# An early ScalarE table load, smaller room bounds in the first mixer, and a final norm in place

## The chip, the cores and the metric

The kernel runs on one core of a Trainium2 chip, in one launch. The metric is the device time of that launch in microseconds (us). Inputs are laid out for the kernel on the host before the launch, and outputs are put back in the reference's order after it.

The core's engines are TensorE (PE in the profile, with PEld for its weight loads), VectorE (DVE), ScalarE (ACT), GpSimd (POOL) and SyncE (SP). SP does no arithmetic here: it issues nearly all transfers. Each engine runs its own list of instructions in order, and a semaphore wait at the head of a list holds everything behind it.

## The reference

One inference step of a two-layer decoder over 512 prompt tokens and 8 × 8 sample tokens, 576 columns in all, with model width 1024, in float32:

```
layer 0: x += mixer_A_and_B(rmsnorm(x))      # pooling mixer and gated DeltaNet, one input and one output projection
layer 1: x += dilated_window_attention(rmsnorm(x))
each layer: x += attention_into_256_memory_tokens(rmsnorm(x)); x += conv_ffn(rmsnorm(x))
y = rmsnorm(x, g_final) = x * rsqrt(mean(x*x) + 1e-6) * g_final
```

The outputs are y and the new states and caches. Of this the change touches the loading of x at the very start, the order of work in layer 0's mixer, and the last line.

## The kernel before

**Layout.** Activations lie transposed: the 1024 channels are 8 tiles of 128 partitions, and the 576 tokens are columns. `x` is two buffers of four tiles each, [128, 4 × 576]. Work goes in two halves of the columns, `HALF = ((0, 256), (256, 320))`: half 0 is 256 columns wide, half 1 is 320.

**Dense layers.** `dense` multiplies streamed weights with an activation held as two rounded parts, so each product takes three matmuls: high × high, high × low, low × high. A weight unit is 128 × 1024 elements, 512 KB: loaded by SP into `wr` (2 buffers), copied to `wh` by ACT, its remainder put into `wl` by DVE (4 buffers each). The callback `evac` takes each result out of PSUM. After every few matmuls `dense` calls `tick()`; a piece of work handed to `later(n, f)` is emitted n ticks on. At the program's end `flush()` emits what is still pending, in order.

**The norm that follows a residual add.** `res_evac` adds PSUM to `x` on DVE and calls `_Next.put(k, hf)`. That squares the tile on ACT and sums squares on DVE (`squares`). After the eighth tile `sums` adds over the partitions with PE (a product with a matrix of ones), takes the diagonal and the inverse root on DVE in small instructions, and `rows` spreads the result over all partitions with PE and copies it from PSUM to SBUF on ACT as `R`.

**The end.** The last down projection of layer 1 works its final four units with half 1 ahead of half 0. `rows` then calls `final(R, hf)`. For each of 8 tiles it makes `y = x * g * R` in a fresh buffer `y` from the arena: either one DVE instruction or an ACT scaling and a POOL product, and SP sends each tile out on its own. Half 1's tiles are spread over later ticks, in steps of four; half 0's are emitted at once.

**The start.** `build` sets `eps` with DVE, issues the load of the small vectors `vecs` from ACT's queue, then from SP: `x` half 0 (two transfers of four tiles), two weight units, `x` half 1 (two transfers), and constants. ACT then scales and rounds each tile of half 0 (`parts`), casts the two weight units, does the same for half 1 and then squares.

**The arena.** Nearly all buffers come from a software allocator, `_Arena`, over 16 pages: 2 of 4608 elements a partition, and 14 of 2304. A page holds float32 or rounded buffers, not both. `room()` counts free elements. The lanes below count idle pages, a page of 4608 as two. The allocator runs when the program is laid out, on the host, so on the chip these conditions set only the order of instructions and which buffers share an address.

**Layer 0's mixer.** `sched` interleaves five lanes with a filler, in an order planned from a table of engine costs. The filler is the input projection's remaining columns (`cols`), then the projection of the memory tokens (`kv`), then half of the output projection (`outp`). Lanes: `first` (tokens, gates, scan), `second` (preparation of later chunks), `third` (sample tokens; it writes 8 state tiles `o_ss`), `fourth` (rounds the pooling mixer's result into `mh` and `ml`, which `outp` multiplies) and `fifth` (the same for the scan's result, into `oh` and `ol`, which the second half of the output projection multiplies). Some lanes wait for room:

```
second:  "pool" in st or self.room() > PROOM
fourth:  "kv" in st or "mem" in st and idle() >= MXPAGES
fifth:   "outp" in st or idle() >= FPAGES
kv:      idle pages >= KVPAGES
```

`"mem"` is set when the memory tokens have been rounded, `"kv"` when their whole projection has been emitted. The pooling mixer's product `pool_mm` is emitted when the planner holds its operands ready, or after its patience of `POOLW` ticks.

Of the kernel before, what the change touches and what calls it, by code (L numbers as in the profile page):

```python
# [11 lines left out]
AF = mybir.ActivationFunctionType  # L12
OP = mybir.AluOpType
# [3 lines left out]
NEG = -1e30  # L17
L = {'k0': 6.0, 'k3': 2.0, 'k1': 3.0, 'k2': 5.0, 't0': 3.0, 't1': 0.5, 't2': 0.2, 't3': 1.0, 't4': 0.4, 'g0': 0.4, 'g1': 0.5, 'g2': 8.0, 'g3': 1.0, 'g4': 0.4, 'g5': 1.5, 'g6': 1.0, 'v0': 3.0, 'v1': 0.2, 'p0': 0.0, 'p1': 0.8, 'p2': 0.0, 'p3': 1.0, 'p4': 1.5, 'p5': 0.2, 'p6': 0.8, 'p7': 0.2, 'p8': 0.8, 'p9': 0.0, 'p10': 0.1, 'p11': 0.3, 'o0': 1.2, 'o1': 3.6, 'o2': 0.0, 's0': 0.1, 's1': 0.5, 's2': 0.1, 's3': 0.8, 's4': 0.0, 's5': 0.6, 's6': 0.0, 'm0': 2.8, 'm1': 0.5, 'm2': 1.2, 'm3': 0.5}
CF, SC, CT, CA = 0.11, 0.85, 8, 20
KVPAGES = 4  # L20
MXPAGES = 2
XT = 3
FPAGES = 2
XL = 4, 16
XL1 = 4, 12
MET0 = 0.0, 0.0, 0.0, 0.0
# [3 lines left out]
KT = 8  # L30
NTOK = 576
HALF = ((0, 256), (256, 320))
# [271 lines left out]
SPARE = 2  # L304
AGE = 40
SROOM = 5500
PROOM = 8000
MROOM = 4500
KROOM = 4000
MRAW = 170  # L310
# [1 line left out]
WROOM = 1500  # L312
OUT_LATER = 24
PATIENCE = 60
POOLW = 40
LOAD_LATER = 18
LOW_LATER = 18
QUICK = 3, 5
# [322 lines left out]
class _Next:  # L641
# [8 lines left out]
    def put(self, k, hf):  # L650
        if not self.last:
            self.parts(k, hf)
        self.squares(k, hf)

    def parts(self, k, hf, lag=True):
        p = self.p
# [27 lines left out]
    def rows(self, hf):  # L684
        p = self.p
        t0, N = HALF[hf]
        if self.R is None:
            self.R = p.S([128, NTOK], s="R1")
        p.nc.scalar.copy(self.R[:, t0:t0 + N], p.rstd_rows(self.y[hf], N)[:, :N])
        if self.on_rows is not None:  # L690
            self.on_rows(self.R, hf)
            if hf == 1 and not self.last:
                self.R = None

    def clear(self):
# [6 lines left out]
class _Prog:  # L702
# [37 lines left out]
        bs = [self.S([128, min(4, n - k) * NTOK], dt, s=name) for k in range(0, n, 4)]  # L740
        return [_Cols(bs[k // 4], k % 4 * NTOK, NTOK) for k in range(n)]

    def load_x(self, src, at=(0, NTOK), eng=None):

        t0, N = at
        if self.x is None:
            self.x = self.wide("x", dt=F32)
        for k in range(0, KT, 4):
            b = self.x[k].buf[:].rearrange("p (k t) -> p k t", k=4)
            (eng or self.nc.sync).dma_start(b[:, :, t0:t0 + N], src[k:k + 4, :, t0:t0 + N].rearrange("k p t -> p k t"))  # L750

    def room(self):
        return self.arena.room()
# [287 lines left out]
    def build(self):  # L1041
        nc, aps = self.nc, self.aps
        c = self.cpool
        self.vecs = c.tile([128, NVEC], F32, name="vecs")
        cid = c.tile([128, 256], F32, name="cid")
        self.my = c.tile([128, 2], F32, name="my")
        self.mR = c.tile([128, 256], F32, name="mR")
        self.y4 = c.tile([128, 4], F32, name="y4")
        self.eps = c.tile([128, 1], F32, name="eps")
        nc.vector.memset(self.eps[:], EPS)  # L1050
        self.acc = {}
        nc.scalar.dma_start(self.vecs[:], aps["vec"])
        self.x = None
        self.load_x(aps["x"], HALF[0])
        self.ident, self.ones = cid[:, 0:128], cid[:, 128:256]


        w, w6 = aps["w"], aps["w6"]
        self.pos = {}
        k = 0  # L1060

        def add(name, n):
            nonlocal k
            self.pos[name] = len(self.stream)
            for _ in range(n):
                self.stream.append((w[k], 1024))
                k += 1

        def tail(l):
            add(f"mq{l}", 8)  # L1070
            add(f"mo{l}", 8)
            for ci, (s, n) in enumerate(CHUNKS):
                add(f"up{l}{ci}", 2 * n)
                if n == 8:
                    add(f"dn{l}{ci}", 8)
                else:
                    self.pos[f"dn{l}{ci}"] = len(self.stream)
                    for i in range(8):
                        self.stream.append((w6[l, i], n * 128))

        add("in", 20)
        add("mk0", 8)
        add("mv0", 8)
        add("outp", 4)
        add("outd", 4)
        tail(0)
        for g in range(3):
            add(f"v{g}", 4)
        for hp in range(4):
            add(f"qk{hp}", 6)  # L1090
        add("mk1", 8)
        add("mv1", 8)
        add("outc", 4)
        tail(1)


        self.quick = {i for a, b in (("v0", "qk0"), ("mv0", "outp"), ("mv1", "outc"))
                      for i in range(self.pos[a] + 3, self.pos[b] + 3)}
        self.load_to(self.NR)
        self.load_x(aps["x"], HALF[1])  # L1100
        nc.sync.dma_start(cid[:], aps["c_id"])
        self.Kc, self.Vc = {}, {}
        nx = _Next(self, "g_mix", 0)
        for hf in range(2):
            for kt in range(KT):
                nx.parts(kt, hf, False)
            self.split_to(2)
        nx.lags = START
        for hf in range(2):
            for kt in range(KT):  # L1110
                nx.squares(kt, hf, False)
        self.x = None
        nx = self.layer0(nx)
        if self.stop == "l0mix":
            return self.flush()
        nx = self.mem_stage(0, nx)
        if self.stop == "l0mem":
            return self.flush()
        nn = _Next(self, "g_mix", 8, perm=True, on_rows=self.rope_rows)
        nn.lags = (18, 24), (10, 20)  # L1120
        self.ffn(0, nx, nn)
        if self.stop == "l0":
            return self.flush()
        nx = self.layer1(nn)
        if self.stop == "l1mix":
            return self.flush()
        nx = self.mem_stage(1, nx)
        self.ffn(1, nx, _Next(self, None, 0, on_rows=self.final, last=True))
        self.flush()

    def rope_rows(self, R, hf):
# [5 lines left out]
                self.nc.sync.dma_start(self.cs[n][:], self.aps["c_" + n])  # L1137
            self.nc.gpsimd.tensor_tensor(self.cs[n][:, t], self.cs[n][:, t], R[:, t], op=OP.mult)

    def final(self, R, hf):  # L1140
        nc, aps = self.nc, self.aps
        t0, N = HALF[hf]

        def tile(k):
            y = self.S([128, N], s="y")
            x, g, r = self.x[k][:, t0:t0 + N], self.vec("g_final", k), R[:, t0:t0 + N]
            if k < 5 if hf == 0 else k % 2:
                nc.vector.scalar_tensor_tensor(y[:], x, g, r, op0=OP.mult, op1=OP.mult)
            else:
                nc.scalar.activation(x, x, AF.Copy, scale=g)  # L1150
                nc.gpsimd.tensor_tensor(y[:], x, r, op=OP.mult)
            nc.sync.dma_start(aps["y"][k][:, t0:t0 + N], y[:])

        for i, k in enumerate(((5, 0, 1, 6, 2, 3, 7, 4), range(KT))[hf]):
            if hf:
                self.later(1 + 4 * i, lambda k=k: tile(k))
            else:
                tile(k)


    def layer0(self, nx):
        nc, aps = self.nc, self.aps
# [320 lines left out]
        def second():  # L1483
            yield 0, 0, lambda: "gates" in st
            yield from vtok()
            yield 0, 0, lambda: "pool" in st or self.room() > PROOM
            yield from self.dn_prep(QKV, 1, st)
# [16 lines left out]
        def fourth():  # L1504
            yield 0, 0, lambda: "kv" in st or "mem" in st and idle() >= MXPAGES
            mh.extend(self.wide("xh", 4))
# [4 lines left out]
        def fifth():  # L1511
# [8 lines left out]
            self.dn1 = self.d8 = self.sc = self.gl = None  # L1520
            yield 0, 0, lambda: "outp" in st or idle() >= FPAGES
            oh.extend(self.wide("xh", 4))
# [8 lines left out]
        def kv():  # L1531
            yield 0, 0, lambda: sum(len(p) * n // 2304 for n, p in self.arena.idle().items()) >= KVPAGES
            self.mem_ahead()
# [971 lines left out]
```

## Time and profile before

| what | us |
|---|---|
| median of 3 runs | 2044.92 |
| lowest and highest run | 2040.68, 2045.32 |
| the profiled execution, its own time | 2044.57 |
| span of its trace, first to last instruction | 2042.4 |
| PE busy in that span | 1987.4 |

The profile shows one execution. Times in its rows count from the span's first instruction, so the profiled execution's own time is 2.2 us longer than its span. Nearly every instruction carries the same source line, since one helper emits them all; they are told apart by engine, operation, shape and place in time. Arena buffers all appear as `page`, PSUM as `p`.

### The profile page before, as it was taken

Reading aid. Unit: us, or ns where it says so; the run is one execution under the profiler, and the core shown is the slowest. Engines: PE = TensorE matmul, PEld = TensorE weight load, DVE = VectorE, ACT = ScalarE, POOL = GpSimd, SP = SyncE. Lnnn points to the kernel's source line nnn. Section 1 sums busy time; section 2 is a strip of 40 time slices with the busy share of each in tenths; the row PEclk is TensorE's granted clock in tenths of the full one; section 3 lists DMA queues with packets and bytes.
Section 4 is the critical chain, followed back from the end, with each engine's and each line's share of the span. In section 5 each row is a group of like instructions: output and inputs, shape, how many; then the busy total and the mean of one; then the engine's idle time right before and its main releaser. Section 6 shows DMA issues by size and latency. Waiting matters only on the chain.

```text
span 2042.4 us, 40671 instructions
## 1 busy us (share of the span) xinstructions
PE 1987.4 (97%) x16443; PEld 1849.4 (91%) x16443; DVE 1252.5 (61%) x3020; ACT 798.2 (39%) x1674; POOL 264.2 (13%) x570
## 2 busy tenths in 40 slices
PE   6999999999999999999999999999999999999997
PEld 6899877978999999999899888879779999999996
DVE  7686676644577467467516676656545675575575
ACT  5564424333444234234322442455334442342342
POOL 1133121000012012011003222200000021121111
PEclk9999999999999999999999999999999999999998
DMA  4221235555322222222554565675553222222222
GB/s 149 73 66 52 76 114 191 169 188 193 108 66 91 84 82 83 83 83 78 167 165 157 196 203 177 220 246 175 171 196 109 80 83 94 74 83 90 76 72 76
DMA packets 104091, 252.29 MB, mean 124 GB/s; under 512 B 11168, under 2 KB 22048, under 8 KB 103904
## 3 DMA queue, kind: packets, MB, share of 16 engines
q1 hardware_dynamic: 103760, 249.49, 37.8%
q8 instruction: 129, 2.11, 0.4%
q14 instruction: 58, 0.48, 0.1%
q10 hardware_dynamic: 144, 0.22, 0.0%
HBM read 227.70 MB, written 21.96 MB: 122 GB/s over the span
## 4 chain that ended last, share of the span: by engine, by line
PE 87%; DVE 6%; ACT 3%; DMA 3%; issue 1%; POOL 0%; SPq 0%; DVEq 0%; ACTq 0%; POOLq 0%
PE p L630 87%; DVE page L630 4%; ACT page L630 2%; DVE wl L630 1%; DMA wr<-in_w 1%; ACT wh L630 1%; DVE rn L630 1%; DMA page<-in_cmk 1%; DMA out_o_ss<-page 0%; DMA page<-xd 0%; DMA page<-in_x 0%; POOL page L630 0%; ACT L630 0%; SPq L630 0%; DMA xd<-page 0%
## 5 line engine op out<-in xcount | busy, mean ns | idle before, releaser
L630 PE MATMUL p<-page,wh 128*128 128x256 f32 (+1 forms) x7296 | 1101.9, 299 | 18.0 <-ACT wh L630 12.8
L630 PEld LDWEIGHTS p<-page,wh 128*128 128x128 f32 x7296 | 1013.2, 191 | 51.2 <-issue 25.8
L630 PE MATMUL p<-page,wl 128*128 128x256 f32 (+1 forms) x3648 | 589.8, 298 | 0.0
L630 PEld LDWEIGHTS p<-page,wl 128*128 128x128 f32 x3648 | 519.8, 191 | 8.2 <-issue 7.2
L630 DVE TENSOR_TENSOR page<-p,page 128x256 f32<-128x256 f32 (+5 forms) x647 | 241.8, 392 | 322.1 <-PE p L630 235.5
L630 ACT CAST wh<-wr 128x1024 fp32r<-128x1024 f32 (+1 forms) x268 | 274.6, 1028 | 378.2 <-PE p L630 297.4
L630 DVE TENSOR_TENSOR wl<-wr,wh 128x1024 fp32r<-128x1024 f32 (+1 forms) x268 | 332.9, 1245 | 83.2 <-ACT wh L630 76.4
L630 DVE SCALAR_TENSOR_TENSOR page<-page,vecs,page 128x256 f32<-128x256 f32 (+4 forms) x545 | 283.8, 526 | 97.5 <-ACT page L630 86.6
L630 PE MATMUL p<-page,page 64*64 64x64 f32 (+13 forms) x3768 | 280.7, 297 | 10.6 <-DVE page L630 4.0
L630 ACT ACTIVATE page<-page,vecs 128x256 f32<-128x256 f32 (+5 forms) x319 | 168.6, 537 | 231.9 <-DVE page L630 226.0
L630 PEld LDWEIGHTS p<-page,page 64*64 64x64 f32 (+6 forms) x3768 | 184.0, 130 | 69.5 <-issue 20.7
L630 POOL COPY page<-page 128x16 f32<-128x16 f32 (+5 forms) x312 | 128.5, 436 | 732.4 <-DVE page L630 732.4
L630 ACT ACTIVATE page<-page 128x256 f32<-128x256 f32 (+6 forms) x293 | 115.8, 410 | 139.1 <-DVE page L630 132.8
L630 POOL TENSOR_TENSOR page<-page,page 128x320 f32<-128x320 f32 (+6 forms) x96 | 91.7, 963 | 446.1 <-DVE page L630 321.8
L630 ACT COPY page<-p 128x256 f32<-128x256 f32 (+8 forms) x161 | 62.5, 413 | 162.4 <-PE p L630 159.9
L630 PE MATMUL p<-wh,page 128*128 128x512 f32 (+1 forms) x368 | 119.1, 397 | 0.0
L630 DVE TENSOR_TENSOR page<-page,page 128x256 fp32r<-128x256 f32 (+8 forms) x181 | 81.5, 463 | 57.4 <-ACT page L630 56.4
L630 DVE TENSOR_TENSOR page<-page 128x256 f32<-128x256 f32 (+5 forms) x222 | 97.9, 454 | 14.6 <-POOL page L630 9.4
L630 ACT CAST page<-page 128x256 fp32r<-128x256 f32 (+2 forms) x118 | 50.1, 439 | 126.0 <-DVE page L630 126.0
L630 PEld LDWEIGHTS p<-wh,page 128*128 128x128 f32 (+1 forms) x368 | 77.3, 223 | 14.5 <-issue 2.5
L630 PE MATMUL p<-cid,page 128*128 128x128 f32 (+3 forms) x669 | 78.3, 258 | 5.6 <-ACT page L630 4.0
L630 POOL MEMSET page<- 128x2 f32 (+4 forms) x110 | 12.2, 111 | 530.6 <-PE p L630 281.8
(84 smaller groups left out, 808.3 us busy)
## 6 DMA issues: line engine op xcount, KB each, us to landing
wr<-in_w SPq DMA_DIRECT2D x252, 512.0 KB, 3.6
page<-in_ck SPq DMA_DIRECT2D x72, 256.0 KB, 5.1
page<-in_cv SPq DMA_DIRECT2D x72, 256.0 KB, 4.4
page<-in_cmk SPq DMA_DIRECT2D x64, 256.0 KB, 5.0
page<-in_cmv SPq DMA_DIRECT2D x64, 256.0 KB, 4.8
wr<-in_w SPq DMA_DIRECT2D x16, 384.0 KB, 3.1
xd<-page SPq DMA_DIRECT2D x16, 288.0 KB, 4.3
out_o_v<-page SPq DMA_DIRECT2D x12, 256.0 KB, 4.5
```

Of the source, the lines that this page charges most:

```text
L630: return f(*args, **kw)
```

## The change

At the start, a one-column copy of `eps` on ACT stands ahead of the load of `vecs` on the same queue, and `x` half 0 comes in four transfers of two tiles in place of two of four. In the mixer five bounds change. At the end, tiles are scaled by `g_final` in place by ACT as soon as they are squared (`scaled`), and `final` multiplies pairs of tiles by the row of inverse roots, in place, and sends a pair in one transfer. For half 0 three pairs take that row from PSUM on DVE and one takes a copy in SBUF on POOL; for half 1 all four pairs take the SBUF copy on DVE, in steps of three ticks.

```diff
-KVPAGES = 4
-MXPAGES = 2
+KVPAGES = 3
+MXPAGES = 1
-FPAGES = 2
+FPAGES = 1
-PROOM = 8000
+PROOM = 6000
-POOLW = 40
+POOLW = 56
...
         self.squares(k, hf)
+        if self.last:
+            self.p.scaled(k, hf)
...
     def rows(self, hf):
         p = self.p
         t0, N = HALF[hf]
+        if self.last:
+            return p.final(p.rstd_rows(self.y[hf], N), hf)
...
-            if hf == 1 and not self.last:
+            if hf == 1:
                 self.R = None
...
-    def load_x(self, src, at=(0, NTOK), eng=None):
+    def load_x(self, src, at=(0, NTOK), n=4):
...
-        for k in range(0, KT, 4):
-            b = self.x[k].buf[:].rearrange("p (k t) -> p k t", k=4)
-            (eng or self.nc.sync).dma_start(b[:, :, t0:t0 + N], src[k:k + 4, :, t0:t0 + N].rearrange("k p t -> p k t"))
+        for k in range(0, KT, n):
+            b = self.x[k].buf[:].rearrange("p (k t) -> p k t", k=4)[:, k % 4:k % 4 + n]
+            self.nc.sync.dma_start(b[:, :, t0:t0 + N], src[k:k + n, :, t0:t0 + N].rearrange("k p t -> p k t"))
...
         nc.vector.memset(self.eps[:], EPS)
+        nc.scalar.copy(self.T([128, 1], "warm")[:], self.eps[:])
         self.acc = {}
         nc.scalar.dma_start(self.vecs[:], aps["vec"])
         self.x = None
-        self.load_x(aps["x"], HALF[0])
+        self.load_x(aps["x"], HALF[0], 2)
...
-        self.ffn(1, nx, _Next(self, None, 0, on_rows=self.final, last=True))
+        self.ffn(1, nx, _Next(self, None, 0, last=True))
...
-    def final(self, R, hf):
+    def scaled(self, k, hf):
+
+        x = self.x[k][:, HALF[hf][0]:sum(HALF[hf])]
+        self.nc.scalar.activation(x, x, AF.Copy, scale=self.vec("g_final", k))
+
+    def final(self, ps, hf):
+
         nc, aps = self.nc, self.aps
         t0, N = HALF[hf]
-
-        def tile(k):
-            y = self.S([128, N], s="y")
-            x, g, r = self.x[k][:, t0:t0 + N], self.vec("g_final", k), R[:, t0:t0 + N]
-            if k < 5 if hf == 0 else k % 2:
-                nc.vector.scalar_tensor_tensor(y[:], x, g, r, op0=OP.mult, op1=OP.mult)
+        R = self.S([128, N], s="R1")
+        nc.scalar.copy(R[:], ps[:, :N])
+
+        def tiles(k, eng, r):
+            x = self.x[k].buf[:].rearrange("p (k t) -> p k t", k=4)[:, k % 4:k % 4 + 2, t0:t0 + N]
+            eng.tensor_tensor(x, x, r.unsqueeze(1).to_broadcast([128, 2, N]), op=OP.mult)
+            nc.sync.dma_start(aps["y"][k:k + 2, :, t0:t0 + N].rearrange("k p t -> p k t"), x)
+
+        for i, k in enumerate(range(0, KT, 2)):
+            if hf:
+                self.later(1 + 3 * i, lambda k=k: tiles(k, nc.vector, R[:]))
+            elif k == 2:
+                tiles(k, nc.gpsimd, R[:])
             else:
-                nc.scalar.activation(x, x, AF.Copy, scale=g)
-                nc.gpsimd.tensor_tensor(y[:], x, r, op=OP.mult)
-            nc.sync.dma_start(aps["y"][k][:, t0:t0 + N], y[:])
-
-        for i, k in enumerate(((5, 0, 1, 6, 2, 3, 7, 4), range(KT))[hf]):
-            if hf:
-                self.later(1 + 4 * i, lambda k=k: tile(k))
-            else:
-                tile(k)
+                tiles(k, nc.vector, ps[:, :N])
```

## Rows read from the trace of the kernel before

**Rows 1.** The page, busy time of PE.

```profile
PE 1987.4 (97%) x16443; PEld 1849.4 (91%) x16443; DVE 1252.5 (61%) x3020; ACT 798.2 (39%) x1674; POOL 264.2 (13%) x570
```

**Rows 2.** Stretches, mixer: engines' busy us (count), granted clock, DMA share, GB/s.

```profile
274.00:282.00 8.00, 6.36 (x33) 5.01 (x32) 4.36 (x13) 1.39 (x2) 1.14 (x2) 0.81 0.84 269
...
336.00:344.00 8.00, 4.26 (x17) 2.62 (x16) 6.10 (x15) 6.33 (x16) 0.33 (x1) 0.99 0.90 283
344.00:350.00 6.00, 5.66 (x23) 5.07 (x24) 3.48 (x10) 1.44 (x5) 0.00 (x0) 0.50 0.79 301
350.00:356.00 6.00, 6.00 (x45) 6.00 (x44) 2.23 (x4) 1.05 (x1) 0.00 (x0) 0.95 0.63 218
```

**Rows 3.** Timeline, mixer's end: start, us, instruction, [idle before <-releaser].

```profile
339.52 0.91 PE L630 MATMUL p<-page,wh 128*128 128x256 f32 x2 [1.07 <-ACT page L630]
...
341.80 0.85 PE L630 MATMUL p<-page,wh 128*128 128x256 f32 x2 [1.36 <-ACT page L630]
```

**Rows 4.** Timeline of the start.

```profile
0.73 0.44 ACTq L630 DMA_DIRECT2D vecs<-in_vec  x1
0.74 1.01 SPq L630 DMA_DIRECT2D page<-in_x  x2
...
5.66 1.28 ACT L630 ACT_TABLE_LOAD   x1 [5.66 <-DMA page<-in_x]
...
6.95 3.30 ACT L630 ACTIVATE page<-page,vecs 128x256 fp32r<-128x256 f32 x8
...
10.16 1.98 ACT L630 CAST wh<-wr 128x1024 fp32r<-128x1024 f32 x2
...
12.04 3.72 ACT L630 ACTIVATE page<-page,vecs 128x320 fp32r<-128x320 f32 x8
```

**Rows 5.** Transfers, first 20 us: count, KB each, us from issue to landing.

```profile
page<-in_x SPq DMA_DIRECT2D x2, 640.0 KB, 9.1
...
vecs<-in_vec ACTq DMA_DIRECT2D x1, 214.5 KB, 3.7
```

**Rows 6.** Timeline of the end.

```profile
2018.42 0.37 DVE L630 TENSOR_SCALAR rn<-rn 128x3 int32<-128x3 int32 x2
...
2022.95 0.42 DVE L630 TENSOR_TENSOR page<-p,page 128x256 f32<-128x256 f32 x1
...
2025.07 0.42 DVE L630 TENSOR_TENSOR page<-p,page 128x256 f32<-128x256 f32 x1 [0.79 <-PE p L630]
...
2028.20 0.42 ACT L630 ACTIVATE page<-page 128x256 f32<-128x256 f32 x1 [3.47 <-DMA out_y<-page]
2028.23 1.48 DVE L630 SCALAR_TENSOR_TENSOR page<-page,vecs,page 128x320 f32<-128x320 f32 x3 [2.73 <-DMA out_y<-page]
...
2028.67 0.70 PE L630 MATMUL p<-page,cid 128*128 128x256 f32 x2 [3.20 <-ACT page L630]
...
2030.28 0.98 DVE L630 TENSOR_SCALAR rn<-rn 128x2 int32<-128x2 int32 x2
...
2033.08 1.22 PE L630 MATMUL p<-cid,rn 128*128 128x128 f32 x4 [3.71 <-DVE rn L630]
...
2034.74 3.48 DVE L630 SCALAR_TENSOR_TENSOR page<-page,vecs,page 128x256 f32<-128x256 f32 x5 [1.72 <-ACT page L630]
```

**Rows 7.** Transfers of y: issue ns min/median/max, first and last start; landing.

```profile
L630 SPq DMA_DIRECT2D out_y<-page x16: 332/399/452, 2025.3 to 2039.6; - x16
...
DMA to landing us min/median/max: 1.7/1.8/1.9
```

**Rows 8.** Groups by shape, 512-column products: count | busy us, mean ns | idle.

```profile
L630 DVE TENSOR_TENSOR page<-page,page 128x512 f32<-128x512 f32 x4 | 4.1, 1022 | 0.1
...
L630 DVE TENSOR_TENSOR page<-p,page 128x512 f32<-128x512 f32 x4 | 2.7, 682 | 0.0
...
L630 POOL TENSOR_TENSOR page<-page,page 128x512 f32<-128x512 f32 x17 | 23.7, 1416 | 54.1 <-DVE page L630 25.7 <-ACT page L630 19.2 <-PE p L630 9.2
```

**Rows 9.** Timeline of the sample lane: PE after POOL waited for a state tile.

```profile
277.17 1.12 PE L630 MATMUL p<-page,page 64*128 64x512 f32 x2 [1.64 <-POOL page L630]
```

## The prediction

> **What bounds the kernel now.** I read the page first. PE is busy for 1987.4 us, 97% of the span [rows 1], so a saving counts only where PE waits, or where nothing is left for PE to do. I looked for such places where the diff touches the program, by stretches, and then read the timeline of each.
>
> The first is the start: PE gets nothing before ACT has scaled half 0 and cast the first weights. ACT stands still until 5.66 us, when a table load of 1.28 us begins that was released by the transfer of `x` [rows 4].
>
> The second is the end of layer 0's mixer. From 336 to 344 us PE runs 17 matmuls, and from 344 to 350 us 23 at a granted clock of 0.50, which is the lower level, 1.2 GHz. The next 6 us hold 45 at 0.95 [rows 2]. The first matmuls of `outp` wait 1.07 and 1.36 us for ACT [rows 3], which is only then rounding the pooling mixer's result: the work of lane `fourth`.
>
> The third is the end of the kernel. The residual add of the last tile starts at 2025.07 us, yet its square starts at 2028.20 us, 3.47 us of idle time before it, released by an outgoing `y` [rows 6]. Its square buffer takes an address that a `y` tile is still being sent from. DVE waits for the same reason. Then come the inverse roots, the row at 2033.08 us, five products on DVE, and eight transfers, the last issued at 2039.6 us [rows 6, 7].
>
> **The start: 0.5 us.** With the copy on `eps`, the table load needs no `x` and can begin at about 0.9 us. It ends near 2.2 us, and the copy near 2.4 us, so `vecs`, on the same queue, is issued 1.6 us later than at 0.73. Its landing took 3.7 us [rows 5], so it lands at about 6.0 us. That is now what half 0's scaling waits for, since two tiles land before four did. Scaling starts at 6.1 us against 6.95 and lasts 3.2 us to the casts' start at 10.16 [rows 4]; the casts take 1.98 us and would end at 11.2. Half 1 of `x` lands 9.1 us after its issue [rows 5], the middle of two transfers that were issued near 3.2 us, right behind two weight units: 12.3 us, and the first of them, I estimate, 0.8 us sooner, at 11.5. The bytes ahead of it are the same after, so half 1 starts at 11.5 against 12.04: 0.5 us of the 0.85 are left. SP has two more issues at about 0.5 us each ahead of the weights (two took 1.01 us [rows 4]); they lie under transfers already queued. Bounds: 0 if half 1 lands 0.5 us later, 0.9 if it lands early. The eight squares and the norm behind half 1 follow without PE, so the shift carries on.
>
> One page speaks against this step. The Trainium skill, ScalarE: Activation LUTs, section "What ACT_TABLE_LOAD costs", adds a drain of about 1.38 us to the load, 2.66 us together. By it `vecs` would be issued another 1.4 us later; here the first scaling follows the load's end by 0.01 us, so the trace shows no drain.
>
> **The mixer: 4.5 us.** Five bounds move, and I follow the allocator through the program before. `second` asks for room when 10,176 elements are free: above 8000 and above 6000. `kv` asks when 6 pages are idle: above 4 and above 3. `fifth` finds 6. So `PROOM`, `KVPAGES` and `FPAGES` alter nothing in that order. `POOLW` matters for one of four products: the last pooling product is emitted because its patience of 40 ticks ran out, and with 56 it comes a few ticks later. PE showed no wait there, so I cost it at nothing; what it can do is shift later decisions of the planner.
>
> `fourth` is the one that waits. `idle()` is 1 from the end of the memory tokens' rounding (near 226 us) until `first` ends, when it becomes 2. With a bound of 1 it may start about 100 us earlier. But it takes two pages, `mh` and `ml`, so it needs the shifted plan to leave two where this one left one. I take that as the likelier case, and price the other below. Its 8 copies on ACT and 8 subtractions on DVE then lie beside the memory projection, which keeps PE busy, and `outp` starts without waiting for them.
>
> What that gives: the two waits, 1.07 + 1.36 = 2.4 us [rows 3]. And the slow stretch: 23 matmuls at the later rate of 45 per 6 us take 3.1 us, so 2.9 us are lost there [rows 2]. Together 5.3. Of the 2.9 I take 2.1, since the transfers' share is already 0.90 and 0.79 there [rows 2] and may hold a weight unit. Sum 4.5. Bounds: 0, and 8.7 us, if all 40 matmuls between 336 and 350 us ran at the later rate (14 − 40 × 6/45).
>
> **The end: 3.2 us.** No `y` buffer is left, so nothing waits for an outgoing tile. What is late next is DVE. Between the sixth tile's add, which ends at 2023.37 us, and the last add stand four pair products of half 1 and one sum of squares. A product of 256 columns takes 0.42 us [rows 6] and one of 512 takes 0.68 [rows 8], so 640 columns take about 0.81. Four with one sum of 0.42, less an overlap of about 0.08 each, make 3.25 us. The last add then ends at 2027.1 us (before, 2025.5), its square at 2027.6 (before, 2028.62), PE's sum 0.70 us on at 2028.3. Before, the reduction that follows had to wait for three products that end at 2029.71 [rows 6]: 1.4 us gained, less overlap 1.3.
>
> In the chain of roots, two instructions took 0.98 us beside POOL's products; the same two for half 1 took 0.37 with POOL idle [rows 6]. After the change POOL is idle there: 0.6. So the row starts 1.9 us earlier, at 2031.2, and ends at 2032.4 (1.22 us [rows 6]).
>
> Three pairs on DVE take 0.68 us each [rows 8] with overlap 1.9 us, to 2034.3. POOL's pair starts 0.45 us after the row, as the first product did before (2034.74 against 2034.3), and takes 1.4 [rows 8], to 2034.3 too. SP sends the first pair at 2033.1, waits for POOL's as second, and issues the last at about 2035.3 against 2039.6. Transfers are twice as long: 0.4 us more each at 301 GB/s [rows 2], three in a row, so 1.1 of the 4.3 us go back: 3.2 us. The 16 scalings that ACT gets replace 7, on an engine that PE does not wait for here except behind the last square. Bounds 2.0 (products do not overlap, transfers of 256 KB land 1 us later) and 4.3.
>
> **Sum.** 0.5 + 4.5 + 3.2 = 8.2. From the profiled execution's own 2044.57 that is 2036.4; the median of the runs is 0.35 above it, so 2036.7 us, 0.40% faster. I take 0.3%, 6.1 us, as what a measurement of this kernel can tell from no change; the three runs before spread over 4.6.
>
> **The rivals.**
> *The mixer's order stays* (0.29): `fourth` still starts when `first` ends, because no two pages are idle sooner. For it: one page idle over the whole stretch, two needed. Then 0.5 + 3.2 = 3.7 are left: 2041.2 us, no change that can be told.
> *State tiles in the way* (0.10): `fourth` takes its pages early, the sample lane's buffers fall on addresses that a state tile is still being sent from, and POOL and PE wait. One such wait is there before: PE lost 1.64 us [rows 9], and the clock fell to 0.81 for 8 us [rows 2], 1.5 us more; 3.1 in all. There are eight tiles. With five such waits 15.5 us go against the 8.2: 2052.2 us, slower. It decides from three waits on, and is slower by over 0.3% from five.
> *POOL and DVE block each other at the end* (0.08): products with both inputs in SBUF took 1.02 us beside POOL against 0.68 from PSUM [rows 8]; if the three pairs go as the first, DVE ends 1.0 us later and so do the transfers: 2037.7. The Trainium skill, SBUF — State Buffer, section "SBUF: two separate sides", says that only products with two SBUF inputs shut POOL out; that is the case of half 1's pairs, when POOL rests.
> *The copy brings no table* (0.04): the load stays ahead of the first scaling, but behind two tiles in place of four, so the gain is between 0 and 0.5: 2037.2 at 0.
> *A drain behind the load* (0.03): scaling starts at 7.5 us, the casts end at 12.7, half 1 starts 0.7 late in place of 0.5 early: 2037.9.
> My forecast, early rounding with all terms, has 0.46.
>
> **How the numbers follow.** The forecast's own range is 2031.5 to 2040: below, 8.7 + 4.3 + 0.4 = 13.4; above, a mixer gain of 1.5. To hold 8 in 10 the range must reach past 2041.2, to 2043.0 (the unchanged mixer with 0 at the start and 2.0 at the end). Left out are the state tiles' waits and a part of the edges. Faster: most of the forecast (0.40) and of the three small rivals (0.11), 0.01 from the unchanged mixer: 0.52. Slower: 0.08, nearly all from the state tiles. Same: 0.40.
>
> **What would show it.** A table load before 2 us, scaling of half 0 near 6.1 us and half 1 near 11.5 us. ACT's rounding of the pooling result between 226 and 330 us, no PE wait ahead of `outp`, and no stretch at clock 0.50 behind it. At the end no wait for `out_y`, the last square near 2027 us less the earlier gains, 8 transfers in place of 16, the last issued 4 us sooner. The prediction is wrong if the rounding still stands behind `first`, or if the sample lane shows several waits for `out_o_ss`.

## The result

| runs | median us | lowest, highest | ratio to before, 95% interval |
|---|---|---|---|
| before, first measurement | 2044.12 | 2040.68, 2045.32 | |
| changed kernel | 2032.20 | 2026.74, 2034.29 | 0.994 [0.9917, 0.9964] |
| changed kernel, measured again | 2032.56 | 2027.73, 2033.18 | 0.9936 [0.9924, 0.9948] |

The change makes the kernel 11.9 us faster, 3.7 us more than the forecast of 8.2; the time lies 0.7 us above the lower end of the range, 2031.5. The first profiled execution of the changed kernel, shown here, is the lowest of its four times (2026.74 us). So the spans of the two first profiles, 17.4 us apart, overstate the gain; why executions of one program differ by so much is the subject of experiment 9.

Busy time and stretches of the changed kernel answer to [rows 1, 2]. The page first, then the windows (busy us and count of each engine, granted clock, DMA share, GB/s):

```profile
PE 1977.3 (98%) x16443; PEld 1840.5 (91%) x16443; DVE 1250.5 (62%) x3018; ACT 803.9 (40%) x1684; POOL 255.5 (13%) x564
```

```profile
274.00:282.00 8.00, 8.00 (x57) 6.65 (x56) 7.27 (x22) 1.05 (x1) 3.02 (x2) 1.00 0.66 195
336.00:344.00 8.00, 8.00 (x61) 8.00 (x60) 5.62 (x14) 3.56 (x8) 0.00 (x0) 1.00 0.98 348
344.00:350.00 6.00, 6.00 (x48) 6.00 (x47) 3.62 (x8) 1.71 (x3) 0.00 (x0) 1.00 1.01 375
350.00:356.00 6.00, 6.00 (x47) 6.00 (x47) 3.65 (x8) 1.05 (x1) 0.00 (x0) 1.00 0.91 316
```

None of these stretches has a low clock any more, and 336 to 350 us hold 109 matmuls against 40. ACT rounds the pooling result a hundred microseconds sooner, and `outp` starts without a wait. First ACT's timeline, before and then in the changed kernel, then PE's in the changed kernel (compare [rows 3]):

```profile
339.07 1.42 ACT L630 CAST page<-page 128x256 fp32r<-128x256 f32 x4
```

```profile
231.88 0.77 ACT L630 CAST page<-page 128x256 fp32r<-128x256 f32 x2
...
233.50 1.42 ACT L630 CAST page<-page 128x256 fp32r<-128x256 f32 x4
...
240.41 0.77 ACT L630 CAST page<-page 128x256 fp32r<-128x256 f32 x2
```

```profile
332.25 0.39 PE L630 MATMUL p<-wh,page 128*128 128x512 f32 x1
332.47 1.11 PE L630 MATMUL p<-page,wh 128*128 128x256 f32 x8
```

The start of the changed kernel answers to [rows 4]; the last line is from the view of who waited for whom on SP's queue, 0 to 20 us (us in total, times, longest), where the kernel before shows no such wait:

```profile
0.73 1.28 ACT L630 ACT_TABLE_LOAD   x1 [0.73 <-PEq L2503]
0.74 1.97 SPq L630 DMA_DIRECT2D page<-in_x  x4
...
0.91 0.38 ACTq L630 DMA_DIRECT2D vecs<-in_vec  x1
2.02 0.19 ACT L630 COPY warm<-eps 128x1 f32<-128x1 f32 x1
2.75 0.94 SPq L630 DMA_DIRECT2D wr<-in_w  x2
3.74 1.30 SPq L630 DMA_DIRECT2D page<-in_x  x2
4.72 1.70 ACT L630 ACTIVATE page<-page,vecs 128x256 fp32r<-128x256 f32 x4 [2.50 <-DMA vecs<-in_vec]
...
9.51 1.04 ACT L630 CAST wh<-wr 128x1024 fp32r<-128x1024 f32 x1 [0.36 <-DMA wr<-in_w]
...
12.68 3.73 ACT L630 ACTIVATE page<-page,vecs 128x320 fp32r<-128x320 f32 x8 [0.78 <-DMA page<-in_x]
```

```profile
SPq L630 <- DMA page<-in_x: 1.3, 3, 0.9
```

Half 0's scaling starts 2.2 us sooner, but half 1's starts 0.64 us later: it now waits for `x`, whose first transfer lands at 12.66 us (11.45 before).

The end answers to [rows 6, 7] (timeline, then the transfers of `y`):

```profile
2009.14 3.37 DVE L630 TENSOR_TENSOR page<-page,page 128x640 f32<-128x640 f32 x5
...
2012.43 0.42 DVE L630 TENSOR_TENSOR page<-p,page 128x256 f32<-128x256 f32 x1
...
2012.88 0.42 ACT L630 ACTIVATE page<-page 128x256 f32<-128x256 f32 x1 [2.84 <-DVE page L630]
...
2017.05 1.22 PE L630 MATMUL p<-cid,rn 128*128 128x128 f32 x4 [3.00 <-DVE rn L630]
2018.31 0.37 ACT L630 COPY page<-p 128x256 f32<-128x256 f32 x1 [4.47 <-PE p L630]
2018.71 1.88 DVE L630 TENSOR_TENSOR page<-page,p 128x512 f32<-128x512 f32 x3 [1.72 <-ACT page L630]
2018.76 1.27 POOL L630 TENSOR_TENSOR page<-page,page 128x512 f32<-128x512 f32 x1 [46.51 <-ACT page L630]
```

```profile
L630 SPq DMA_DIRECT2D out_y<-page x8: 372/384/442, 2010.0 to 2021.1; - x8
```

The last square follows its add by 0.45 us (3.1 before), the row by 4.6 (8.0), the span's end by 12.5 (17.3).

**Where the time went.** The stretches between weight casts can be compared over all profiles of this study, 13 in all, each counted by whether it has the old or the new form of the part (left out of a row are the profiles with only some of its edits, or with others). Lowest to highest, in us:

| stretch | old form | new form | forecast |
|---|---|---|---|
| start to the third cast | 33.7 to 34.2 (6) | 34.0 to 34.4 (3) | 0.5 less |
| third to 21st cast, by the form of the mixer | 131.8 to 134.4 (7) | 131.8 to 134.9 (6) | none |
| 21st to 53rd cast (rest of the mixer and beyond) | 302.0 to 304.0 (6) | 290.6 to 293.7 (6) | 4.5 less |
| 53rd to 161st | 776.3 to 776.7 | 776.4 to 776.7 | none |
| 161st to 201st | 333.7 to 335.3 (7) | 334.4 to 337.5 (6) | none |
| 201st to 261st | 387.9 | 387.9 | none |
| 261st to the span's end | 72.2 to 72.4 (6) | 69.0 to 69.1 (4) | 3.2 less |

By the medians of the rows the start costs 0.3 us, the mixer gives 10.9, the end 3.2. The 161st to 201st give back some 1.4; see experiment 9. The third to the 21st spread by 3 us in either form, and their medians differ by 0.6.

### The profile page after: what moved, and what is told of

Same layout as the page of the kernel before. It is cut to its first block, busy times and chain, and to the rows that moved or that the text cites. A ratio compares the mean times of both kernels' runs of the same rounds, so it can differ in the third digit from the quotient of the medians.

```text
span 2025.0 us, 40655 instructions
## 1 busy us (share of the span) xinstructions
PE 1977.3 (98%) x16443; PEld 1840.5 (91%) x16443; DVE 1250.5 (62%) x3018; ACT 803.9 (40%) x1684; POOL 255.5 (13%) x564
## 5 line engine op out<-in xcount | busy, mean ns | idle before, releaser
L630 DVE SCALAR_TENSOR_TENSOR page<-page,vecs,page 128x256 f32<-128x256 f32 (+4 forms) x536 | 278.4, 524 | 94.8 <-ACT page L630 85.5
L630 PE MATMUL p<-page,page 64*64 64x64 f32 (+10 forms) x3776 | 278.4, 296 | 9.3 <-DVE page L630 4.5
L630 ACT ACTIVATE page<-page,vecs 128x256 f32<-128x256 f32 (+5 forms) x328 | 174.0, 537 | 236.7 <-DVE page L630 225.1
L630 PEld LDWEIGHTS p<-page,page 128*32 128x32 f32 (+6 forms) x3776 | 181.2, 129 | 71.0 <-issue 21.3
L630 POOL TENSOR_TENSOR page<-page,page 128x256 f32<-128x256 f32 (+6 forms) x89 | 84.7, 957 | 442.6 <-DVE page L630 283.9
L630 DVE TENSOR_TENSOR page<-page,page 128x256 fp32r<-128x256 f32 (+10 forms) x185 | 84.4, 468 | 62.9 <-ACT page L630 61.8
```

What stands on the lines that cost most here:

```text
L630: return f(*args, **kw)
```

## The experiments

Ratios and medians of a run stand against runs of the kernel before on the same chip.

**1. Which bound moves the mixer.** The kernel before, with

```diff
-POOLW = 40
+POOLW = 56
```

> The kernel before with POOLW alone raised from 40 to 56; MXPAGES stays at 2, and the start and the end stay as before. In the program that this gives, two pages are idle when the memory tokens' rounding ends, so fourth's bound of 2 is met there already. My theory: POOLW alone makes the whole gain of the mixer. ACT's rounding of the pooling result stands between 226 and 245 us, the first matmuls of outp wait for nothing, no stretch near 344 to 350 us has a granted clock of 0.50, and POOL waits for no state tile near 276 us. By the idle time and clock that PE loses before in these places (3.9 us idle and 3.4 us by the clock at outp, 3.1 us at the state tile) the span falls by 10 to 11 us, the median to about 2034. Rival, as the prediction had it: the lower bound MXPAGES is what lets fourth start, POOLW gives nothing: rounding stays behind first, near 339 us, and the median stays within 1 us of 2044.

Measured: 2033.43 us against 2044.47, ratio 0.995 [0.9937, 0.9963], 11.0 us. The rounding stands at 233 us, `outp` waits for nothing (ACT's and PE's timeline):

```profile
233.04 0.77 ACT L630 CAST page<-page 128x256 fp32r<-128x256 f32 x2
```

```profile
333.45 1.11 PE L630 MATMUL p<-page,wh 128*128 128x256 f32 x8
```

With `POOLW` at 56 two pages are idle when `fourth` first asks, so `MXPAGES` may be 2 or 1: the changed kernel with `MXPAGES`, `PROOM`, `KVPAGES` and `FPAGES` put back comes out as the same program. With `POOLW` at 40 and `MXPAGES` at 1 there is no program: `fourth` starts early and finds a page for `mh` but none for `ml`. One bound of five does the work; that it can be 44, 48 or 52 as well (the same program as 56) shows that it only has to outlast the wait of the last pooling product.

**2. The new plan, with the rounding held back.**

```diff
-POOLW = 40
+POOLW = 56
-MXPAGES = 2
+MXPAGES = 3
```

> The kernel before with POOLW raised to 56 and MXPAGES raised to 3, so that fourth again starts only when first ends, in a plan whose buffers lie where the changed kernel has them until then. Theory of two causes: the state tile's wait near 276 us goes with the shifted plan (3.1 us), and the waits and the low clock at the entry of outp stay (7.2 us): median about 2041. Rival A, only the early rounding counts, and the state tile's wait goes because fourth takes its pages early: the wait near 276 us stays, median within 1 us of 2044. Rival B, the early rounding counts for nothing: median about 2033, with the entry of outp as slow as before.

Measured: 2042.77 us, ratio 0.9992 [0.9984, 1.0001], 1.7 us less, which the interval does not tell from none. From the 21st to the 53rd cast the trace takes 301.9 us, 1.3 less than the old form's median. PE's wait of [rows 9], 1.64 us behind POOL and a state tile, is gone; POOL's own wait for that tile is down from 1.97 us to 0.27 (POOL's timeline, before and in this run):

```profile
276.08 1.03 POOL L630 TENSOR_TENSOR page<-page,page 64x512 f32<-64x512 f32 x1 [1.97 <-DMA out_o_ss<-page]
```

```profile
274.70 1.03 POOL L630 TENSOR_TENSOR page<-page,page 64x512 f32<-64x512 f32 x1 [0.27 <-DMA out_o_ss<-page]
```

So that wait goes with the plan that `POOLW` at 56 gives, and not with the early rounding; whether by other addresses or by another order was not tried apart. By this one profile it is worth a little over a microsecond, not the 3.1 expected, and the times do not show it. The rest, 9.3 us between the medians of the two runs, is the early rounding. It falls at the entry of `outp`: counted from the 21st weight cast, the two runs are 0.1 us apart at the 40th, 8.7 at the 44th and 10.2 at the 53rd. What the early rounding removes stands in the windows and PE's timeline of this run, and in the windows of experiment 1's run (last fence):

```profile
336.00:344.00 8.00, 4.87 (x15) 3.28 (x16) 6.77 (x18) 6.43 (x18) 0.00 (x0) 0.79 0.91 294
344.00:350.00 6.00, 6.00 (x34) 6.00 (x34) 2.17 (x4) 0.20 (x1) 0.00 (x0) 0.71 0.66 224
```

```profile
336.52 0.84 PE L630 MATMUL p<-page,wh 128*128 128x256 f32 x2 [1.07 <-ACT page L630]
338.80 0.84 PE L630 MATMUL p<-page,wh 128*128 128x256 f32 x2 [1.43 <-ACT page L630]
340.13 0.39 PE L630 MATMUL p<-page,wh 128*128 128x256 f32 x1 [0.49 <-ACT page L630]
```

```profile
336.00:344.00 8.00, 8.00 (x62) 7.82 (x61) 4.90 (x13) 4.01 (x8) 0.41 (x1) 1.00 1.02 334
344.00:350.00 6.00, 6.00 (x47) 6.00 (x46) 3.81 (x9) 1.14 (x3) 0.00 (x0) 1.00 1.03 401
```

The 14 us hold 49 matmuls with late rounding and 109 with early. Two matmuls of 256 columns take 0.84 us here; eight take 1.11 in the changed kernel. PE is fed tile by tile as ACT and DVE round, so it is slow even where it counts as busy. Over the 21st to 53rd cast, late against early rounding (these two runs) differ by 5.1 us in PE's idle time, by 1.5 in the low clock (3.2 at `outp` against 1.7 near 209 us), and by 3.6 in busy time that the clock does not explain.

**3. The end alone.** The changed kernel with the five bounds put back and the start as before.

```diff
-MXPAGES = 1
+MXPAGES = 2
-POOLW = 56
+POOLW = 40
...
-        nc.scalar.copy(self.T([128, 1], "warm")[:], self.eps[:])
...
-        self.load_x(aps["x"], HALF[0], 2)
+        self.load_x(aps["x"], HALF[0])
```

> The kernel before with the last norm's edits alone: tiles scaled in place by ACT, products by pairs from PSUM, one transfer for a pair; the start and the five bounds are those of before. Theory: the end gains by itself what it gained in the changed kernel, from the start of the last residual add to the span's end 13.2 us in place of 17.3, median 3.5 to 4 us lower, about 2040.4. Rival: the end's gain hangs on the earlier phases (where the tiles lie, which transfers are under way), then it is under 2 us here.

Measured: 2039.51 us, ratio 0.9976 [0.9966, 0.9986], 5.0 us. From the last add to the span's end it takes 12.4 us and from the 261st cast 69.0, as in the changed kernel: the end's gain does not hang on the rest. The trace gives 3.2 us for it, at the edge of what the times say.

**4. In place alone.** The kernel before without the `y` buffer, single tiles and sixteen transfers kept.

```diff
-            y = self.S([128, N], s="y")
...
-                nc.vector.scalar_tensor_tensor(y[:], x, g, r, op0=OP.mult, op1=OP.mult)
+                nc.vector.scalar_tensor_tensor(x, x, g, r, op0=OP.mult, op1=OP.mult)
...
-                nc.gpsimd.tensor_tensor(y[:], x, r, op=OP.mult)
+                nc.gpsimd.tensor_tensor(x, x, r, op=OP.mult)
```

> The kernel before with one edit: the last norm writes its products in place into x, so there is no y buffer and nothing waits for an outgoing tile; single tiles, their order, the engines and the sixteen transfers stay. Theory: the last square follows its residual add at once (before, 2.7 us behind it), then DVE's reduction still waits for products of half 1; of the end's gain of 4 us (start of the last add to the span's end 17.3 us before, 12.4 with all of the end's edits) 1.5 to 2 us come from this alone, so that stretch takes about 15.5 us, and the rest from pairs and half as many transfers. Rival: all of it comes from the pairs, because the order of the work on DVE sets the reduction's start anyway: 17 us.

Measured: 2042.80 us, ratio 0.9987 [0.9976, 0.9998], 2.0 us. The trace takes 69.8 us from the 261st cast, 2.4 less than before, and 14.9 from the last add to the span's end, 0.6 less than expected; the square no longer waits for a transfer:

```profile
2024.36 0.42 DVE L630 TENSOR_TENSOR page<-p,page 128x256 f32<-128x256 f32 x1 [0.79 <-PE p L630]
...
2024.70 2.51 DVE L630 SCALAR_TENSOR_TENSOR page<-page,vecs,page 128x320 f32<-128x320 f32 x3
2024.82 0.42 ACT L630 ACTIVATE page<-page 128x256 f32<-128x256 f32 x1 [0.80 <-DVE page L630]
...
2027.13 0.28 DVE L630 CUSTOM_DVE_ANT_0 page<-p,cid 128x128 f32<-128x128 f32 x1
```

Three quarters of the end's gain are the wait for outgoing tiles; the products of half 1 still stand ahead of the reduction at 2027.13. The other edits of the end together (pairs, half as many transfers, scaling on ACT, the row from PSUM) make the other 0.8.

**5. The start alone.** The kernel before with the copy and the four transfers.

```diff
+        nc.scalar.copy(self.T([128, 1], "warm")[:], self.eps[:])
...
-        self.load_x(aps["x"], HALF[0])
+        self.load_x(aps["x"], HALF[0], 2)
```

> The kernel before with the start's edits alone: a copy of one column from eps ahead of the loads, and half 0 of x in four transfers of two tiles. As the prediction had it: half 1's scaling starts at 11.5 us against 12.04, and the third weight cast comes 0.5 us sooner than before (34.18 us). My theory from the changed kernel's profile: the table load is early and vecs lands near 4.6 us, but the two more issues on SP's queue put the first weights and half 1 of x back by about 1.1 us, so half 1's scaling starts near 12.7 us and the third cast 0.2 to 0.4 us later than before. The median tells neither: within 1 us of 2044 by both.

Measured: 2045.89 us, ratio 1.0004 [0.9995, 1.0014]. Half 1's scaling starts at 12.27 us and the third cast at 34.04, in the middle of the old form's 33.7 to 34.2. The 0.5 us of the forecast are not there.

**6. Half 0 in two transfers again.** The changed kernel with

```diff
-        self.load_x(aps["x"], HALF[0], 2)
+        self.load_x(aps["x"], HALF[0])
```

> The changed kernel, but half 0 of x comes in two transfers of four tiles, as before; the copy from eps stays ahead. Theory: the two more issues on SP's queue are what put half 1 of x back, so with two transfers half 1 lands near 11.4 us again while the table load is early: half 0's scaling starts near 5.5 us, half 1's near 11.4 us, and the third weight cast comes near 33.5 us (34.44 in the changed kernel, 34.06 in the run with the end's edits alone). Rival: half 1's landing is set by the bytes ahead of it and not by the issues; then half 1 starts near 12.3 us as in the changed kernel, and the third cast does not move. The median, about 1 us lower than the changed kernel's, tells neither.

Measured: 2028.17 us, ratio 0.9926 [0.9913, 0.9938]. ACT's timeline:

```profile
5.80 3.30 ACT L630 ACTIVATE page<-page,vecs 128x256 fp32r<-128x256 f32 x8 [3.59 <-DMA page<-in_x]
9.01 1.98 ACT L630 CAST wh<-wr 128x1024 fp32r<-128x1024 f32 x2
11.68 3.73 ACT L630 ACTIVATE page<-page,vecs 128x320 fp32r<-128x320 f32 x8 [0.69 <-DMA page<-in_x]
```

Half 0 starts a microsecond later than in the changed kernel, half 1 a microsecond sooner, and the third cast comes at 33.34 us (33.32 and 33.18 in the two runs of experiment 8): 0.5 sooner than the old form's median, 0.8 sooner than the changed kernel's. So splitting half 0 into four transfers did the harm. With it SP issues the first weights 0.96 us and half 1 0.75 us later than before (2.75 against 1.79 us, 3.74 against 2.99); transfers of half the size come with it, and the two were not tried apart.

**7. Four transfers without the copy.** One run.

```diff
-        self.load_x(aps["x"], HALF[0])
+        self.load_x(aps["x"], HALF[0], 2)
```

> The kernel before with half 0 of x in four transfers of two tiles and without the copy from eps. Theory: the table load is released by the landing of the first two tiles, near 4.2 us, half 0's scaling starts near 5.5 us; half 1 lands near 12.2 us as in the run with both of the start's edits, so the third cast stands where it is there (34.0 us, within 0.3): the copy is worth nothing beside four transfers, since half 1 of x is what is late. Rival: the copy is worth 0.5 us by the third cast.

Measured: 2045.18 us (before 2044.80), third cast at 35.03 us, outside both. `x` itself came late here (half 1 was scaled from 13.25 us), so what the copy is worth beside four transfers stays open.

**8. Four products on DVE at the end,** on top of experiment 6: the row goes to SBUF for half 1 only, and half 0 is

```diff
-            elif k == 2:
-                tiles(k, nc.gpsimd, R[:])
             else:
                 tiles(k, nc.vector, ps[:, :N])
```

> As the run before (two transfers of four tiles for half 0 of x), and at the end of half 0 all four pair products run on DVE straight from PSUM: the copy of the row to SBUF and POOL's product are left out there. Theory: in the changed kernel DVE's first product starts only when ACT's copy of the same row has ended, 0.40 us behind the row; without the copy it starts 0.04 us behind the row, and four products of 0.63 us end 2.55 us behind it, against 2.28 in the changed kernel, but the first three transfers are issued sooner and the last one at about the same time or 0.2 us sooner. From the row's start to the span's end 7.7 to 8.0 us (7.95 in the changed kernel). Rival: the first product still starts 0.40 us behind the row, for another reason than ACT's copy; then the end is 0.3 us longer.

Measured: 2026.70 us, ratio 0.9914 [0.99, 0.9927]. In the timeline the first product starts 0.03 us behind the row, so ACT's copy of the same PSUM tile was what held it:

```profile
2019.34 1.22 PE L630 MATMUL p<-cid,rn 128*128 128x128 f32 x4 [3.01 <-DVE rn L630]
2020.59 2.48 DVE L630 TENSOR_TENSOR page<-page,p 128x512 f32<-128x512 f32 x4 [1.31 <-PE p L630]
```

From the row to the span's end it takes 7.44 us (7.91 in the changed kernel), a little better than expected. Then both kernels on one chip:

> Two transfers for half 0 of x and four products on DVE at the end, beside the changed kernel on one chip. Theory: the start gives 1.1 us by the third cast (33.3 against 34.4) and the end 0.3 to 0.4 us, so the median is 1 to 2 us below the changed kernel's. Rival, as the medians of the separate runs have it (2026.7 and 2032.2): 5 us.

Measured: 2030.01 us, ratio 0.9923 [0.9909, 0.9937], 2.5 us below the changed kernel. This lies a little beyond the 1 to 2 us expected and far from the rival's 5. The intervals overlap; the traces show 0.8 us at the start by the medians and 0.4 at the end, and the 5 us of the separate runs did not come again. This version is the better of the two by what the traces show; how much in the median is not settled.

**9. The same programs once more.**

> The changed kernel once more, beside the next run. Theory: the first profiled execution of it (2026.7 us) was one with little low clock; in this one the same waits stand at the same places (1.7 us ahead of the second matmuls near 34 us, 3.2 us near 87 us), and what differs by a few us is how long the clock stays at 0.50 behind them. The start, the entry of outp and the end take what they took: third cast near 34.4 us, no wait at outp, 12.5 us from the last add to the span's end. Rival: the difference to the median lies in a part that the change touched. Median 2031 to 2033.

> The kernel before once more. Theory: the waits stand where they stood (1.7 us ahead of 34 us, the state tile's near 277 us, 1.07 and 1.36 us at the entry of outp), the low clock behind the first two comes in some executions and not in others, and behind the entry of outp it comes again, since the waits there follow each other. Rival: the clock falls behind the same waits in each execution of the same program; then it stands at 0.50 for some us right behind 34 us and near 280 us, as in the first profile.

Measured: 2032.56 us for the changed kernel and one run of 2042.47 for before. The windows of before, first profile (34 to 40 us; for 274 to 282 see [rows 2]), then second:

```profile
34.00:40.00 6.00, 4.74 (x22) 4.74 (x23) 4.68 (x8) 2.15 (x3) 0.56 (x3) 0.50 0.38 124
```

```profile
28.00:34.00 6.00, 3.69 (x24) 2.98 (x22) 4.76 (x23) 1.84 (x5) 0.34 (x2) 1.00 0.01 1
34.00:40.00 6.00, 5.05 (x42) 5.05 (x43) 4.97 (x9) 2.08 (x3) 0.88 (x6) 1.00 0.43 137
...
274.00:282.00 8.00, 6.19 (x43) 3.96 (x42) 4.57 (x15) 2.17 (x5) 1.03 (x1) 1.00 0.75 254
```

In the first profile 34 to 40 us had a clock of 0.50 and 22 matmuls, and 274 to 282 had 0.81. PE waits in the second as in the first: 1.56 us up to 31 us in both, 1.69 us up to 35 us (1.52 in the first, where the clock was low from 33.2 us on), 1.81 us for the state tile (1.64). The clock fell at these waits in one execution and not in the other. The changed kernel shows the same near 1310 us. PE's wait of 1.14 us for DVE ends at 1308.48 us in the first profile and at 1311.91 in the second, so the windows, first and second profile, are 3.43 us apart:

```profile
1305.57:1317.57 12.00, 10.49 (x94) 6.63 (x94) 10.66 (x33) 6.75 (x16) 1.56 (x3) 1.00 0.63 224
```

```profile
1309.00:1321.00 12.00, 10.48 (x74) 6.14 (x74) 9.00 (x24) 5.43 (x13) 1.56 (x3) 0.72 0.65 225
```

The rival falls for these waits. In both profiles of before the low clock follows the entry of `outp`. For the changed kernel the theory holds in part: its two profiles are 5.8 us apart, outside the parts that the change touched, but the low clock is not all of it. The one near 1310 us makes 2.2. Near 115 us the second has a wait of 1.5 us with the low clock behind it that the first has not, and 1.4 us go there; near 390 us it is 1.9 by a longer wait alone (PE's timeline, first and second profile):

```profile
386.85 1.13 PE L630 MATMUL p<-page,cid 128*128 128x256 f32 x4 [0.82 <-DVE page L630]
```

```profile
390.32 1.13 PE L630 MATMUL p<-page,cid 128*128 128x256 f32 x4 [3.15 <-DVE page L630]
```

The low clock near 34 and 87 us, where the theory looked for it, is not in the second profile at all.

## Why the prediction was right, and where it was off

**What bounds the kernel** held in the main: the time came from places where PE waited, but in the mixer a third of it (3.6 us in experiment 2) lies in time that counts as busy.

**The mixer** was right in mechanism and too small. `PROOM`, `KVPAGES` and `FPAGES` alter nothing, as the allocator said. `fourth` did start a hundred microseconds early because "the shifted plan" left two pages. That it would leave two was taken as likelier, not followed through the planner, so here the forecast was lucky. And that plan alone suffices: the lower bound `MXPAGES`, to which I gave the early start, is needed by nothing (experiment 1). The mis-sized term is "the two waits" plus "the slow stretch", 5.3 us, of which I took 4.5. It counted the two longest waits and the one stretch at 0.50, and left out the time between, where PE is busy with single matmuls that wait for rounding. The bound of 8.7 us, all matmuls of 336 to 350 us at the later rate, was the better estimate: the two runs of experiments 1 and 2 differ by 9.3. Taking 2.1 of 2.9 because transfers might hide the rest was the wrong direction; the transfers' share went up to 1.02 there and PE did not wait.

**The state tiles** I had as a risk alone. The new plan took the one such wait away, in place of adding more. A plan that moves buffers can go either way, so it should have stood in the sum's bounds as a gain of up to 3.1 us. By the trace of experiment 2 it is worth a little over 1 us, more in the executions in which the clock falls behind it.

**The end** came out as worked out: 3.2 us forecast, 3.2 in the traces. The three pair products on DVE took 1.88 us (1.9 forecast), POOL's 1.27 (1.4), the last issue came 8.6 us behind the start of the last add (8.6). Two errors cancel inside: DVE's wait of 0.40 us for ACT's copy was not seen, and the last issue, near 2021.1 us, follows the last product by 0.5 us, where I allowed 1.0.

**The start** was wrong in sign, by 0.8 us. Two steps failed. "`vecs`, on the same queue, is issued 1.6 us later": it was issued at 0.91 us, in the middle of the table load, so half 0 started 1.4 us sooner than forecast; this did no harm. And "the bytes ahead of it are the same after, so half 1 starts at 11.5", with the two more issues costed at nothing since "they lie under transfers already queued": the four transfers moved the landings of the first weights and of half 1 of `x` back by 1.1 and 1.2 us, to 9.5 and 12.7, of which 0.96 and 0.75 us are the later issues. Experiment 6 shows it by going back to two. SP's waits of 1.3 us for `x` stand behind the issue of half 1's first transfer, and one of 0.6 us comes in experiment 6 too, so they are not the cause. I had counted the issues and then hidden them; what they hid under had to be issued behind them.

**The rivals.** The order of the mixer did not stay (experiment 1 against 2). DVE and POOL did not block each other at the end: DVE's three products took 0.68 to 0.69 us each, two of them beside POOL's. The 1.02 us of that rival was a mean of two kinds: two of the four products ran with POOL at rest and took 0.68 and 0.69 us, two beside POOL and took 1.07 and 1.64. The table load began at 0.73 us, and the copy followed its end by 0.01: no drain is to be seen. The Trainium skill, ScalarE: Activation LUTs, section "What ACT_TABLE_LOAD costs", adds a drain of about 1.38 us to a load; this trace does not agree with it, and the measurement decides here: of its 19 loads 15 are followed by ACT's next instruction within 0.02 us, and the other four by one that waits for DVE.

## What to carry to other kernels

Where an engine is fed tile by tile, price the whole stretch at the rate of the next steady stretch, not by the sum of the waits that the profile names: busy time there is not work at full rate. Count a transfer's issues on its queue as a delay for everything that is issued behind them; here, in the first microseconds, nothing hid it. Before a set of bounds is credited with a change of order, follow each through the planner: one did all here, and not the one whose name says so.

## What the runs showed of the hardware

At the same wait of the same program TensorE's clock may fall or not. Of the 13 profiles, 4 had a granted clock of 0.50 (the lower level, 1.2 GHz) at the two waits of 1.0 to 1.7 us near 30 and 34 us, in three of them from a point between the two waits and in one behind the second, and 9 had not. At the wait of 3.2 us near 87 us 12 of 13 had it, from within the wait on; behind the state tile's wait of 1.1 to 1.8 us 2 of the 6 that have this wait; behind the wait of 1.1 us near 1310 us 9 of 13. At the entry of `outp` all 7 with late rounding had it, and none of the 6 with early. In one or two profiles each it came near 115, 209 and 389 us too, behind waits of 1.5 to 2.8 us.

Counted as PE's busy time by the part of the clock that is missing, each costs 1.4 to 3.4 us. What it costs in time differs from place to place. Between two profiles of one program it was 2.1 us near 34 us and 2.2 near 1310, but little near 87: the changed kernel's first profile had the low clock there and its second had not, and their weight casts stand equally far apart ahead of it and behind it (0.29 us at the 11th, 0.30 at the 15th); before's two profiles, with 1.5 and 2.9 us of it there by that count, part by 0.6. The stretches without such places repeat to 0.4 us in 776 and to 0.1 in 388. So executions differ by a few microseconds through the clock and through waits of different length, and a wait that is taken away also takes away a chance of the low clock behind it. Behind the wait near 1310 us the runs with early rounding lost up to 3.4 us by that count and those with late rounding at most 1.7; whether that is chance is open, and it is where the 1.4 us that the changed kernel gives back appear.

ACT's queue issued a DMA at 0.91 us, 0.18 us into a table load that took 1.28; what it held back was ACT's next instruction, which started at 2.02 us.
